# The first stage of a streaming-encoder step: shifts and scales by quarters of the channels, index keys made in it, and a gate with four weight buffers

## The chip, the cores and the metric

One core of a Trainium2 chip runs the whole step as one program. The metric is the time of one execution on the device in microseconds; 1285.39 is the median of three runs of the kernel before.

## The reference

One layer (DEPTH 1) over 1024 prompt tokens and 32 sample tokens, D = 1024 channels, everything in float32. What the change touches is the beginning and one factor at the end:

```
mod = silu(c) @ w_ada + b_ada                  # c: one row for the prompt, one for the sample
shift, scale, gate = split(mod, 3)
h = rms_norm(x, g_norm) * (1 + scale) + shift
z = h @ w_in                                   # columns: q k v gate_a iq iw ik glu gate_b merge
dots = relu(iq . ik); score = sum_heads(iw * dots); top-k keys per query; attention over them
...
x = x + gate * (mixed @ w_out); y = rms_norm(x, g_final)
```

Besides y it returns k, v, ik (the index keys) and the last rows of the convolution, for both token groups.

## The kernel before

Activations are held with channels on the partitions: xT, and h as a pair hh + hl (the rounded value and the rest), 8 blocks k of 128 channels by 1056 tokens. A product in float32 precision is three matmuls, wh by hh, wh by hl and wl by hh (mm3).

The **first stage** makes hh and hl and the first index queries. What runs in it, and in which order, stands in two lists. LOADS is the order of the loads on SP's queue: x:i is a tile of 128 tokens (x:8 the 32 sample tokens, 4 buffers), a a piece of w_ada (tiles of 1 MB, 4 buffers), q and k raw weights. ORDER is the order in which the rest is issued; PE, DVE and ACT are scheduled by hand, POOL and SP are not. Its words:
- sq:i squares x tile i with its sum (ACT, sq_x); sc:i,.. puts the small operations that turn sums into 1/rms on a list (scale_x: ACT's root between DVE's small operations, then the scaling of the tile on the engine that XENG names: tile 4 on ACT, tiles 0, 7 and 8 on POOL, the others on DVE). Two of that list are issued after each word (DRIP), all that are left before a t.
- t:i transposes tile i (8 on PE, trans_x), c:i copies the result to xT, half on DVE, half on ACT.
- m:q,i,k multiplies the 4 columns of silu(c) with block k of w_ada, for half q of the channels, i = 0 shift, 1 scale (mod); p:q,i,k,e prepares such a block as a split pair, which makes its matmuls two short ones (mod_pre); v copies a row out of PSUM, o turns it by transposes and makes AB, the scale and shift per channel (mod_row, mod_out).
- h:part,k makes hh and hl of channel block k for tokens f (0 to 255), i (256 to 767) or t (768 to 1023): h on POOL, hh on ACT, hl = h - hh on DVE (h_of); hS does it for the 32 sample tokens on DVE.
- w splits 128 columns of index-query weights (prep); q:t,c,k multiplies query tile t (two heads each) with column group c (512 or 288 columns) of block k.

Behind ORDER the two query tiles are copied out of PSUM (iq_out) and the **jobs** begin (class Jobs): one after another, a block of weight columns times all of hh and hl, 8 steps each; proj has 9 matmuls of 352 columns a step. The first job before is the index keys and head weights (72 columns), the second query tiles 2 and 3. After each step the job loop issues entries of the list side, npop of them per step (side work: transposes, the dots of the indexer, and at the end the gate). idx_done copies the index keys out, writes them twice with their split (dup), transposes them (tr) and puts the first dots on the list. The caches' keys are loaded and transposed by cache_ik ahead of the first job and by cache_kT as a side entry.

Near the end the jobs yaj multiply with w_a (8 tiles of 128 channels), with the **gate** as side work: 16 additions gate_add on DVE (each a scaled 128 x 512 block of w_ada for both token groups), then for either half a split and a row by matmuls (gate_row). The blocks are loaded by POOL's queue into 2 buffers, graw; gate_add(i) issues the load of i + 2. Its rate is 0.25 entries a step in the first of the four weight loads and 0.375 in the others. Then comes the output product y, which takes all of PSUM.

Of the kernel before, what the change touches and what calls it, by code (L numbers as in the profile page):

```python
# [107 lines left out]
def _build(tc, nc, a, o, top):  # L108
# [121 lines left out]
    def load_ada(q, i, k0, n=4):  # L230

        c = D * i + 512 * q
        src = w_ada[128 * k0:128 * k0 + 512, c:c + 512].rearrange("(k p) c -> p k c", p=128)
        t = tl(stp, [128, 4, 512], F, "ada", 4)
        for k in range(0, 4, n):
            nc.sync.dma_start(t[:, k:k + n], src[:, k:k + n])
        for k in range(4):
            ada[q, i, k0 + k] = t[:, k]
# [23 lines left out]
    nc.vector.memset(rest, 0.0)
    psS, psS_st = pool("psS", space=PSUM)
    p = tl(psS, [128, 512], F, "iq00")
    for i in range(WARM):
        nc.tensor.matmul(p, rest[:, 0:128], rest, start=True, stop=True)
    nc.vector.memset(scf, 0.0)
# [4 lines left out]
    nc.scalar.activation(sc, p.rearrange("p (s k) -> p k s", s=2), AF.Silu)  # L272
# [63 lines left out]
    pm, mrow, halves = {}, {}, {}  # L336

    def mod_pre(q, i, k, eng):
        h = tl(stp, [128, 512], FR, "ah", 2)
        l = tl(stp, [128, 512], FR, "al", 2)  # L340
        (nc.vector.tensor_copy if eng >= 2 else nc.scalar.copy)(h, ada[q, i, k])
        (nc.gpsimd if eng % 2 else nc.vector).tensor_sub(l, ada[q, i, k], f32(h))
        halves[q, i, k] = h, l

    def mod(q, i, k):

        if k == 0:
            pm[q, i] = misc([4, 512])
        out = pm[q, i]
        if (q, i, k) in halves:  # L350
            h, l = halves.pop((q, i, k))
            nc.tensor.matmul(out, sch[:, k, :], h, start=k == 0, stop=False)
            nc.tensor.matmul(out, scz[:, k, :], l, start=False, stop=k == KD - 1)
        else:
            nc.tensor.matmul(out, scf[:, k, :], ada[q, i, k], start=k == 0, stop=k == KD - 1)  # L355

    def mod_row(q, i):
        mrow[i] = tl(stp, [128, 512], F, "h", 4)[:4]
        (nc.scalar.copy, nc.vector.tensor_copy)[i](mrow[i], pm.pop((q, i)))

    def mod_out(q):
        p = misc([128, 2, 4, 4])
        for i in range(2):
            for c in range(4):
                nc.tensor.transpose(p[:, i, c, :], mrow[i][:, 128 * c:128 * c + 128], ident[:4, :4])
        j = slice(4 * q, 4 * q + 4)
        mc = tl(stp, [128, 2, 4, 2], F, "mc", 2)
        bias = bg_[:, 0:16].rearrange("p (i j) -> p i j", i=2)[:, :, j, None]
        nc.vector.tensor_add(mc, p[:, :, :, 2:4], bias.to_broadcast([128, 2, 4, 2]))
        nc.vector.tensor_add(AB[:, j, 2:4], p[:, 1, :, 0:2], mc[:, 1])  # L370
        nc.vector.tensor_mul(AB[:, j, 2:4], AB[:, j, 2:4], bg_[:, 16:24][:, j, None].to_broadcast([128, 4, 2]))
        nc.vector.tensor_add(AB[:, j, 0:2], p[:, 0, :, 0:2], mc[:, 0])

    def h_of(j, sel_):
        x, hi, lo = sel_(xT[:, j]), sel_(hh[:, j]), sel_(hl[:, j])
        h = tl(stp, [128, 512], F, "h", 4)[:, :x.shape[-1]]
        nc.gpsimd.tensor_scalar(h, x, AB[:, j, 2:3], AB[:, j, 0:1], op0=OP.mult, op1=OP.add)  # L377
# [3 lines left out]
    def h_sample():  # L381
        h = tl(stp, [128, 512], F, "h", 4)[:, :KD * TS].rearrange("p (k n) -> p k n", k=KD)
        z = slice(TP, T)
        nc.vector.tensor_mul(h, xT[:, :, z], AB[:, :, 3:4].to_broadcast([128, KD, TS]))
        nc.vector.tensor_add(h, h, AB[:, :, 1:2].to_broadcast([128, KD, TS]))
        nc.vector.tensor_copy(hh[:, :, z], h)
        nc.vector.tensor_sub(hl[:, :, z], h, f32(hh[:, :, z]))
# [3 lines left out]
    def iq_mm(t, w, ks, cs=(0, 1)):  # L391
        for k in ks:
            for c in cs:
                if k == 0 and c not in iqps[t]:
                    iqps[t][c] = tl(psS, [128, 512], F, f"iq{t}{c}")
# [3 lines left out]
                    k == 0, k == KD - 1)  # L399

    iqw = {}
    drip = []
    for op, *i in ORDER:
# [4 lines left out]
        elif op == "p":  # L408
            mod_pre(*i)
# [15 lines left out]
        elif op == "w":  # L425
            iqw[i[0]] = prep(iqraw, 128 * i[0], 128)
        elif op == "h":
            h_of(i[1], lambda x, z=part_of[i[0]]: x[:, z])
        elif op == "hS":
            h_sample()  # L430
        elif op == "q":
            iq_mm(i[0], iqw[i[0]], [i[2]], (i[1],))
        elif op == "sch":
            split(sc, sch[:, :, 0:2], sch[:, :, 2:4])
            nc.scalar.copy(scz[:, :, 0:2], sc)
# [4 lines left out]

    idv = ident.rearrange("p (a b) -> p a b", a=4)
    nc.gpsimd.tensor_add(sel[:, 0], idv[:, 0], idv[:, 1])
    nc.gpsimd.tensor_add(sel[:, 1], idv[:, 2], idv[:, 3])
    nc.gpsimd.tensor_add(sel[:, 0], sel[:, 0], sel[:, 1])
    for i in range(1, 4):
        nc.gpsimd.tensor_copy(sel[:, i], sel[:, 0])

# [80 lines left out]
    def first_w():  # L528
        h, l = [slot8(FR)[:, :KD * 72].rearrange("p (k n) -> p k n", k=KD) for i in range(2)]
        split(ikraw[:, :, :72], h, l)  # L530
        return h, l

    iq_out(0, (0,))
    first = first_w()
    iq_out(0, (1,))
    iq_out(1)
# [14 lines left out]
    class Jobs:  # L551
# [29 lines left out]
        def run(self):  # L581
# [27 lines left out]
            if evac:  # L609
# [3 lines left out]
    psS_st.close()  # L613
    psA, psA_st = pool("psA", space=PSUM)
# [748 lines left out]
    jobs = [("w", [(w_in, C_IK, 64), (w_in, C_IW, 8)], [(0, 72, idx_done)], 1, hrows),  # L1363
# [111 lines left out]
    yaj = Jobs([("w", [(a["w_a"][0], 128 * j, 256)], [(0, 128, ya_done(j)), (128, 128, ya_done(j + 1))], 0.375 if j else 0.25,  # L1475
# [95 lines left out]
    def gate_add(i):  # L1571
# [8 lines left out]
        gate_load(i + 2)  # L1580
# [149 lines left out]
```

## Time and profile before

| what | us |
|---|---|
| median of 3 runs (1285.0 to 1286.13) | 1285.39 |
| profiled execution | 1284.44 |
| its span | 1282.6 |
| TensorE busy | 1253.7 (98%) |
| DVE busy | 899.9 (70%) |
| ACT busy | 616.6 (48%) |
| POOL busy | 196.8 (15%) |

Busy shares are means over stages with different limits; TensorE's matmuls are pipelined, and their ends are modelled. The time of an instruction is its duration on its engine, x8 a run of eight put together; what ended the idle time before it stands in brackets. Groups put like instructions together.

### The profile page before, as it was taken

What the parts mean: (1) busy time and instruction counts of PE and PEld (TensorE: products, weight loads), DVE (VectorE), ACT (ScalarE), POOL (GpSimd) and SP (SyncE); (2) the same over time, 40 slices, a digit from 0 to 9 for tenths busy, and PEclk for the clock granted to TensorE, in tenths of its full rate; (3) what the DMA queues carried; (4) which work ended last, traced back from release to release, by engine and by line L of the source; (5) the groups of instructions that cost most, each with busy time, mean ns of one, the idle gap of its engine ahead of it and who ended that gap; (6) DMA issues with size and microseconds to landing.
All of it is one profiled execution on the core that took longest, in us unless ns stands there. A gap on an engine that the chain in (4) does not pass through costs nothing.

```text
span 1282.6 us, 19154 instructions
## 1 busy us (share of the span) xinstructions
PE 1253.7 (98%) x7434; PEld 1179.0 (92%) x7434; DVE 899.9 (70%) x1435; ACT 616.6 (48%) x1142; POOL 196.8 (15%) x289
## 2 busy tenths in 40 slices
PE   7899999999999999999999999999999999998997
PEld 2589999999999999999999999999998889997786
DVE  4855547878899888978875469752358888667454
ACT  5645443576676667666114243340247675115222
POOL 3730110000000000100000000000123352221222
PEclk9999999999999999999999999999999999999999
DMA  9431222131222211211222421266124326545131
GB/s 341 133 101 51 84 76 76 51 101 52 86 69 64 97 56 67 85 67 69 101 101 103 165 101 47 89 235 203 38 86 113 91 77 224 166 152 186 54 127 71
DMA packets 110395, 136.38 MB, mean 106 GB/s; under 512 B 10667, under 2 KB 87715, under 8 KB 110176
## 3 DMA queue, kind: packets, MB, share of 16 engines
q1 hardware_dynamic: 99232, 100.62, 25.0%
q10 hardware_dynamic: 5872, 19.48, 3.8%
q0 software_dynamic: 5200, 15.05, 3.6%
q8 instruction: 58, 0.95, 0.3%
q14 instruction: 33, 0.27, 0.1%
HBM read 98.60 MB, written 36.54 MB: 105 GB/s over the span
## 4 chain that ended last, share of the span: by engine, by line
PE 92%; DVE 2%; DMA 2%; POOL 2%; issue 1%; ACT 1%; ACTq 0%; SPq 0%; DVEq 0%; POOLq 0%
PE proj L545 66%; PE PT L1284 2%; PE y L130 2%; PE y L132 2%; PE y L131 2%; PE O L130 1%; PE O L132 1%; PE O L131 1%; DMA graw<-in_w_ada_dram 1%; PE misc L743 1%; PE misc L744 1%; POOL h L377 1%; PE misc L355 1%; PE misc L132 1%; PE misc L131 1%
## 5 line engine op out<-in xcount | busy, mean ns | idle before, releaser
L967 DVE SCALAR_TENSOR_TENSOR s<-u,vec,s 128x1086 f32<-128x1086 f32 x240 | 314.4, 1346 | 2.6
L545 PE MATMUL proj<-hh,wh 128*128 128x352 f32 x1440 | 312.8, 325 | 0.0
L545 PE MATMUL proj<-hh,wl 128*128 128x352 f32 x1440 | 310.3, 323 | 0.0
L545 PE MATMUL proj<-hl,wh 128*128 128x352 f32 x1440 | 309.8, 323 | 0.0
L545 PEld LDWEIGHTS proj<-hh,wh 128*128 128x128 f32 x1440 | 245.1, 189 | 1.9
L545 PEld LDWEIGHTS proj<-hh,wl 128*128 128x128 f32 x1440 | 246.8, 188 | 0.0
L545 PEld LDWEIGHTS proj<-hl,wh 128*128 128x128 f32 x1440 | 244.6, 188 | 0.0
L813 ACT ACTIVATE relu<-scores,cand 128x384 bf16<-128x384 f32 (+6 forms) x224 | 183.6, 821 | 72.1 <-DVE cand L828 69.5
L127 DVE TENSOR_TENSOR wl<-raw,wh 128x1024 fp32r<-128x1024 f32 (+1 forms) x84 | 100.7, 1202 | 79.6 <-ACT wh L126 78.4
L126 ACT CAST wh<-raw 128x1024 fp32r<-128x1024 f32 (+1 forms) x84 | 85.9, 1026 | 56.2 <-PE proj L545 44.2
L746 ACT ACTIVATE relu<-misc 128x384 f32<-128x384 f32 (+3 forms) x80 | 39.9, 523 | 63.6 <-PE misc L744 62.3
L757 DVE SCALAR_TENSOR_TENSOR scores<-relu,iws,scores 128x384 f32<-128x384 f32 (+3 forms) x70 | 43.6, 655 | 34.5 <-ACT relu L746 34.4
L126 ACT CAST u<-PT 128x512 fp32r<-128x512 f32 (+2 forms) x76 | 43.1, 571 | 45.1 <-PE PT L1284 42.9
L127 DVE TENSOR_TENSOR u<-PT,u 128x512 fp32r<-128x512 f32 (+2 forms) x76 | 50.6, 670 | 14.7 <-ACT u L126 14.3
L906 ACT ACTIVATE s<-proj 128x1056 f32<-128x1056 f32 x24 | 25.3, 1052 | 68.1 <-PE proj L545 68.1
L126 ACT CAST mh<-E 128x1056 fp32r<-128x1056 f32 x8 | 8.6, 1074 | 72.1 <-DVE E L1428 72.1
L813 ACT ACTIVATION_READ_ACCUMULATOR relu<-scores,cand 128x1 f32 x224 | 41.8, 187 | 0.0
L545 PE MATMUL proj<-oa,wh 128*128 128x352 f32 x192 | 41.7, 326 | 0.0
L1264 POOL TENSOR_SCALAR E<-E,st 128x1024 f32<-128x1024 f32 (+4 forms) x36 | 33.5, 932 | 42.0 <-DVE st L1263 22.8
L545 PE MATMUL proj<-u,wh 128*128 128x352 f32 x192 | 38.6, 322 | 0.0
L1259 ACT ACTIVATE E<-E,st 128x1024 f32<-128x1024 f32 (+4 forms) x36 | 34.7, 963 | 7.9 <-DVE st L1252 7.8
L1663 ACT ACTIVATE x<-yv 128x512 f32<-128x512 f32 (+2 forms) x19 | 11.6, 609 | 55.8 <-DVE yv L1662 55.8
(444 smaller groups left out, 2113.8 us busy)
## 6 DMA issues: line engine op xcount, KB each, us to landing
raw<-in_w_in_dram SPq DMA_DIRECT2D x24, 1024.0 KB, 5.3
raw<-in_w_in_dram SPq DMA_DIRECT2D x16, 512.0 KB, 5.2
ada<-in_w_ada_dram SPq DMA_DIRECT2D x24, 256.0 KB, 5.4
sma_d<-s ACTq DMA_DIRECT2D x8, 528.0 KB, 2.7
smb_d<-s ACTq DMA_DIRECT2D x8, 528.0 KB, 2.7
ga_d<-s ACTq DMA_DIRECT2D x8, 528.0 KB, 2.7
qh_d<-s ACTq DMA_DIRECT2D x8, 528.0 KB, 2.7
ql_d<-s SPq DMA_DIRECT2D x8, 528.0 KB, 2.8
```

The costliest lines, as they stand in the source:

```text
L126: nc.scalar.copy(hi, src)
L127: nc.vector.tensor_sub(lo, src, f32(hi))
L130: nc.tensor.matmul(out, ah, bh, start=first, stop=False)
L131: nc.tensor.matmul(out, ah, bl, start=False, stop=False)
L132: nc.tensor.matmul(out, al, bh, start=False, stop=last)
L545: nc.tensor.matmul(p[:n, c, :CH], a_[:, k, :n], b_(k, c), start=first, stop=last)
L746: nc.scalar.activation(r[:, :n], p[:, :n], AF.Relu, scale=0.125)
L757: nc.vector.scalar_tensor_tensor(acc, r[:, :n], w, acc, op0=OP.mult, op1=OP.add)
L813: nc.scalar.activation(scr[:, :s.shape[1]], s, AF.Sign, bias=f32(hold["cand"])[:, i:i + 1], accum_out=cnt[:, i:i + 1])
L967: nc.vector.scalar_tensor_tensor(d[:, :DW], u[:, k:k + DW], wj[:, k:k + 1], d[:, :DW], op0=OP.mult, op1=OP.add)
L1259: nc.scalar.activation(e, e, AF.Exp, bias=mn, scale=-1.0, accum_out=st[:, 1:2])
L1264: nc.gpsimd.tensor_scalar(e, e, st[:, 2:3], 1.0, op0=OP.mult, op1=OP.mult)
```

## The change

The shifts and scales are made by quarters of 256 channels. w_ada is loaded in tiles of 4 channel blocks by 2 x 256 columns (shift and scale side by side), 5 buffers. silu(c) is widened to 32 columns (scp, zero beyond the first two), and the four blocks of a tile are multiplied into four groups of 32 partitions of one PSUM bank, which the matmuls with sel in mod_out add while they turn the row. The split pairs (p) are gone. AB comes two channel blocks at a time, and hS as well. The index keys' product (k:, ik_mm) is in ORDER, by column groups of 352; of the index queries only tile 0 is. Tile 1 is the first job. The transposes of x use the two misc banks. idx_done is called ahead of the first job, and the caches' transposes are side entries.

```
 LOADS: x:2 a:0,0 x:3 a:0,1 x:4 x:5 q:0 a:1,0 a:1,1 x:6 x:8 x:7 k a:2,0 a:2,1 x:0 x:1 a:3,0 a:3,1 q:1
 ORDER:
+sq:2 b sc:2 t:2 c:2 m:0,0 sq:3 sc:3 t:3 c:3 m:0,1 v:0 sq:4 sc:4 o:0 t:4 c:4 w:0 sq:5 sc:5 t:5 c:5 h:i,0 h:i,1 q:0,0
+q:0,1 m:1,0 sq:6 m:1,1 v:1 sq:8 sc:6,8 o:1 t:6 t:8 c:6 c:8 h:i,2 sq:7 sc:7 h:i,3 q:0,2 t:7 c:7 h:t,0 hS:0 q:0,3
+h:t,1 hS:1 q:1,0 wk h:t,2 q:1,1 h:t,3 q:1,2 q:1,3 k:0,1,2 m:2,0 k:1,1,2 k:2,1,2 m:2,1 v:2 k:3,1,2 sq:0 o:2 sq:1
+h:i,4 sc:0,1 h:i,5 q:0,4 t:0 c:0 q:0,5 t:1 c:1 m:3,0 h:t,4 hS:2 h:t,5 q:1,4 h:f,0 q:1,5 k:4,1,2 h:f,1 k:5,1,2 h:f,2
+m:3,1 h:f,3 v:3 k:0,0 k:1,0 o:3 h:i,6,1 k:2,0 h:i,7,1 h:t,6 k:3,0 h:t,7 hS:3 h:f,4 q:0,6 h:f,5 q:0,7 q:1,6 q:1,7
+k:6,1,2 h:f,6 k:7,1,2 w:1 h:f,7 k:4,0 k:5,0 k:6,0 k:7,0
...
+    def load_ada(q, g):
+        t = ada[q, g] = tl(stp, [128, 4, 2, 256], F, "ada", 5)
+        for i in range(2):
+            c = D * i + 256 * q
+            nc.sync.dma_start(t[:, :, i], w_ada[512 * g:512 * g + 512, c:c + 256].rearrange("(k p) c -> p k c", p=128))
...
+    def mod(q, g):
+        if g == 0:
+            pm[q] = tl(psS, [128, 512], F, "acc")
+        for j in range(4):
+            nc.tensor.matmul(pm[q][32 * j:32 * j + 32], scp[:, 4 * g + j, :], ada[q, g][:, j].rearrange("p i c -> p (i c)"),
+                             start=g == 0, stop=g == 1)
...
+                nc.tensor.matmul(p[:, i, c, :], mrow[q][:, 256 * i + 128 * c:256 * i + 128 * c + 128], sel[:, 0, 0:2],
+                                 start=True, stop=True)
...
+        (nc.vector if eng else nc.gpsimd).tensor_scalar(h, x, AB[:, j, 2:3], AB[:, j, 0:1], op0=OP.mult, op1=OP.add)
...
+    def ik_mm(k, *cs):
+        wh, wl = iqw["k"]
+        for a_, b_, first, last in ((wh, hh, k == 0, False), (wh, hl, False, False), (wl, hh, False, k == KD - 1)):
+            for c in cs:
+                nc.tensor.matmul(ikp[:72, c, :CH], a_[:, k, :72], b_[:, k, CH * c:CH * c + CH], start=first, stop=last)
...
-    jobs = [("w", [(w_in, C_IK, 64), (w_in, C_IW, 8)], [(0, 72, idx_done)], 1, hrows),
+    jobs = [("w", None, [(0, 128, 1)], 1, hrows),
...
-    cache_ik()
-    side.append(cache_kT)
-    Jobs(jobs, first).run()
+    jobs = Jobs(jobs, iqw[1])
+    jobs.load(1)
+    load_caches()
+    idx_done(ikp)
+    side.extend([cache_ik, cache_kT])
...
-    yaj = Jobs([... 0.375 if j else 0.25, ...
+    yaj = Jobs([... 0.5 if j else 0.25, ...
...
-            graw[i] = tl(mx, [128, 512], F, "graw", 2)
+            graw[i] = tl(at, [128, 512], F, "gt", 2) if i & 2 else tl(mx, [128, 512], F, "graw", 2)
...
-        gate_load(i + 2)
+        if i < 2:
+            gate_load(i + 2)
+        gate_load(i + 4)
```

## Rows read from the trace of the kernel before

**Rows 1.** List of TensorE's waits: us in total, times, longest.
```profile
PE tx L327 <- DVE xt L315: 5.0, 2, 3.2
...
PE y L130 <- ACT qh L1595: 3.8, 1, 3.8
...
PE proj L545 <- ACT wh L126: 2.1, 1, 2.1
```

**Rows 2.** Chain of waits, first 160 us: start, us, what.
```profile
59.31 6.00 POOL h L377 x7
```

**Rows 3.** TensorE in order of time, first stage: start, us, instruction, idle before.
```profile
10.81 1.97 PE L327 MATMUL tx<-ident,xt 128*128 128x128 f32 x8 [3.23 <-DVE xt L315]
...
19.52 1.07 PE L327 MATMUL tx<-ident,xt 128*128 128x128 f32 x8
...
24.11 1.03 PE L327 MATMUL tx<-ident,xt 128*128 128x128 f32 x8
...
68.22 0.29 PE L132 MATMUL iq<-hh,wl 128*128 128x288 f32 x1
...
69.83 0.41 PE L646 MATMUL misc<-ident,s 128*64 128x128 f32 x2 [1.32 <-DMA s<-in_cache_idx_k_dram]
```

**Rows 4.** ACT in order of time, first stage.
```profile
19.64 1.06 ACT L293 ACTIVATE junk<-xt 128x1024 bf16<-128x1024 f32 x1 [3.66 <-DMA xt<-in_x_prompt_dram]
...
22.64 1.13 ACT L313 ACTIVATE xt<-xt,rs_r 128x1024 f32<-128x1024 f32 x1
...
45.53 0.59 ACT L333 COPY xT<-tx 128x512 f32<-128x512 f32 x1 [2.41 <-PE tx L327]
...
46.02 1.06 ACT L293 ACTIVATE junk<-xt 128x1024 bf16<-128x1024 f32 x1
```

**Rows 5.** Gate weights' tile: who stood idle before it (us, times).
```profile
  DMA graw<-in_w_ada_dram: 15.4, 4
```

**Rows 6.** TensorE in order of time, after 1138 us.
```profile
1144.56 1.08 PE L545 MATMUL proj<-oh,wh 128*128 128x352 f32 x3 [2.07 <-ACT wh L126]
```

**Rows 7.** Stretches: busy us of each engine, granted clock, DMA share, GB/s.
```profile
20.00:30.00 10.00, 10.00 (x42) 3.34 (x40) 6.25 (x18) 8.52 (x17) 5.64 (x5) 1.00 1.04 380
...
1144.00:1148.00 4.00, 3.44 (x12) 3.44 (x13) 4.00 (x6) 0.50 (x1) 2.44 (x3) 0.60 0.75 248
```

**Rows 8.** DVE in order of time, first stage.
```profile
18.62 0.75 DVE L315 TENSOR_SCALAR xt<-xt,rs_r 128x1024 f32<-128x1024 f32 x1
...
21.50 0.15 DVE L306 RECIPROCAL rs_r<-rs_s 128x1 f32<-128x1 f32 x1
...
22.26 0.16 DVE L310 TENSOR_TENSOR rs_r<-rs_r,rs_t 128x1 f32<-128x1 f32 x1
...
36.92 1.61 DVE L315 TENSOR_SCALAR xt<-xt,rs_r 128x1024 f32<-128x1024 f32 x1
```

**Rows 9.** Groups by form, first 160 us: count, busy us, mean ns, idle before.
```profile
L355 PE MATMUL misc<-ada,scf 128*4 128x512 f32 x40 | 20.1, 620 | 0.0
...
L377 POOL TENSOR_SCALAR h<-xT,AB 128x256 f32<-128x256 f32 x16 | 13.4, 850 | 5.7 <-ACT xT L333 5.7
...
L377 POOL TENSOR_SCALAR h<-xT,AB 128x512 f32<-128x512 f32 x8 | 9.4, 1172 | 2.3 <-DVE vv L303 2.0 <-DVE hl L387 0.4
...
L378 ACT ACTIVATE hh<-xT,AB 128x512 fp32r<-128x512 f32 x8 | 6.2, 802 | 0.0
...
L379 DVE TENSOR_TENSOR hl<-h,hh 128x256 fp32r<-128x256 f32 x16 | 7.7, 489 | 4.2 <-POOL h L377 4.2
...
L379 DVE TENSOR_TENSOR hl<-h,hh 128x512 fp32r<-128x512 f32 x8 | 5.8, 735 | 0.6 <-POOL h L377 0.6
```

**Rows 10.** TensorE in order of time, behind the first stage.
```profile
81.77 0.64 PE L545 MATMUL proj<-hh,s 128*72 128x352 f32 x3
...
95.52 0.39 PE L130 MATMUL proj<-hh,wh 128*128 128x512 f32 x1
...
96.61 0.39 PE L130 MATMUL proj<-hh,wh 128*128 128x512 f32 x1
```

More of the change, by code (lines that the diff above doesn't have):

```diff
@@ L228, in _build @@
     xn = {}
[L230 to L238, printed above, removed]
+    def load_ada(q, g):
[3 more added lines that the diff above has]
+            nc.sync.dma_start(t[:, :, i], w_ada[512 * g:512 * g + 512, c:c + 256].rearrange("(k p) c -> p k c", p=128))
     def load_x(i):
@@ L249, in _build @@
     nc.scalar.dma_start(brow[16:24], fold(a["g_norm"]))
-    iqraw = None
+    ikraw, iqraw = [tl(wpool, [128, KD, 256], F, "raw", 2) for i in range(2)]
     for op, *i in LOADS:
@@ L255, in _build @@
             load_ada(*i)
-        elif op == "q":
-            iqraw = load_w([(w_in, C_IQ, 256)])
-        else:
-            ikraw = load_w([(w_in, C_IK, 64), (w_in, C_IW, 8)])
+        elif op == "k":
+            for c, c0, n in ((0, C_IK, 64), (64, C_IW, 8)):
+                nc.sync.dma_start(ikraw[:, :, c:c + n], w_in[:, c0:c0 + n].rearrange("(k p) c -> p k c", p=128))
+        else:
+            c = 128 * i[0]
+            nc.sync.dma_start(iqraw[:, :, c:c + 128], w_in[:, C_IQ + c:C_IQ + c + 128].rearrange("(k p) c -> p k c", p=128))
+    idv = ident.rearrange("p (a b) -> p a b", a=4)
+    nc.gpsimd.tensor_add(sel[:, 0], idv[:, 0], idv[:, 1])
+    nc.gpsimd.tensor_add(sel[:, 1], idv[:, 2], idv[:, 3])
+    nc.gpsimd.tensor_add(sel[:, 0], sel[:, 0], sel[:, 1])
+    for i in range(1, 4):
+        nc.gpsimd.tensor_copy(sel[:, i], sel[:, 0])
     rest = tl(stp, [128, 512], BF, "junk")
@@ L263, in _build @@
     psS, psS_st = pool("psS", space=PSUM)
[L264 to L267, printed above, removed]
+    for tag in ("acc", "iq0", "iq1"):
+        tl(psS, [128, 512], F, tag)
+    ikp = tl(psS, [128, 3, 512], F, "ik")
+    scp = tl(stp, [128, KD, 32], F, "scp")
+    nc.vector.memset(scp, 0.0)
     warm = tl(stp, [128, 1], F, "warm")
@@ L334, in trans_x @@
         cops[i] = copies
[L336 to L355, printed above, removed]
@@ L357, in mod_row @@
-    def mod_row(q, i):
-        mrow[i] = tl(stp, [128, 512], F, "h", 4)[:4]
-        (nc.scalar.copy, nc.vector.tensor_copy)[i](mrow[i], pm.pop((q, i)))
+    pm, mrow = {}, {}
+    def mod(q, g):
[4 more added lines that the diff above has]
+                             start=g == 0, stop=g == 1)
+    def mod_row(q):
+        mrow[q] = tl(stp, [128, 512], F, "h", 4)
+        (nc.scalar.copy, nc.vector.tensor_copy)[q % 2](mrow[q], pm.pop(q))
@@ L361, in mod_out @@
     def mod_out(q):
-        p = misc([128, 2, 4, 4])
+        p = misc([128, 2, 2, 2])
         for i in range(2):
[L364 to L367, printed above, removed]
-        bias = bg_[:, 0:16].rearrange("p (i j) -> p i j", i=2)[:, :, j, None]
-        nc.vector.tensor_add(mc, p[:, :, :, 2:4], bias.to_broadcast([128, 2, 4, 2]))
@@ L370, in mod_out @@
[L370 to L375, printed above, removed]
+            for c in range(2):
+                nc.tensor.matmul(p[:, i, c, :], mrow[q][:, 256 * i + 128 * c:256 * i + 128 * c + 128], sel[:, 0, 0:2],
+                                 start=True, stop=True)
@@ new lines, in mod_out, with h_of @@
+        j = slice(2 * q, 2 * q + 2)
+        mc = tl(stp, [128, 2, 2, 2], F, "mc", 2)
+        bias = bg_[:, 0:16].rearrange("p (i j) -> p i j", i=2)[:, :, j, None]
+        nc.vector.tensor_add(mc, p, bias.to_broadcast([128, 2, 2, 2]))
+        nc.vector.tensor_mul(AB[:, j, 2:4], mc[:, 1], bg_[:, 16:24][:, j, None].to_broadcast([128, 2, 2]))
+        nc.vector.tensor_copy(AB[:, j, 0:2], mc[:, 0])
+    def h_of(part, j, eng=0):
+        z = part_of[part]
+        x, hi, lo = xT[:, j, z], hh[:, j, z], hl[:, j, z]
@@ L376, in h_of, with h_sample @@
         h = tl(stp, [128, 512], F, "h", 4)[:, :x.shape[-1]]
-        nc.gpsimd.tensor_scalar(h, x, AB[:, j, 2:3], AB[:, j, 0:1], op0=OP.mult, op1=OP.add)
+        (nc.vector if eng else nc.gpsimd).tensor_scalar(h, x, AB[:, j, 2:3], AB[:, j, 0:1], op0=OP.mult, op1=OP.add)
         nc.scalar.activation(hi, x, AF.Identity, bias=AB[:, j, 0:1], scale=AB[:, j, 2:3])
         nc.vector.tensor_sub(lo, h, f32(hi))
[L381 to L387, printed above, removed]
+    def h_sample(q):
+        h = tl(stp, [128, 512], F, "h", 4)[:, :2 * TS].rearrange("p (k n) -> p k n", k=2)
+        k, z = slice(2 * q, 2 * q + 2), slice(TP, T)
+        nc.vector.tensor_mul(h, xT[:, k, z], AB[:, k, 3:4].to_broadcast([128, 2, TS]))
+        nc.vector.tensor_add(h, h, AB[:, k, 1:2].to_broadcast([128, 2, TS]))
+        nc.vector.tensor_copy(hh[:, k, z], h)
+        nc.vector.tensor_sub(hl[:, k, z], h, f32(hh[:, k, z]))
@@ L426, in _build @@
             iqw[i[0]] = prep(iqraw, 128 * i[0], 128)
+        elif op == "wk":
+            iqw["k"] = prep(ikraw, 0, 72)
         elif op == "h":
-            h_of(i[1], lambda x, z=part_of[i[0]]: x[:, z])
+            h_of(*i)
         elif op == "hS":
-            h_sample()
+            h_sample(*i)
         elif op == "q":
[L432 to L435, printed above, removed]
+            iq_mm(0, iqw[0], [i[1]], (i[0],))
+        elif op == "k":
+            ik_mm(*i)
         for f in range(DRIP):
@@ L439, in _build @@
     stp_st.close()
[L441 to L446, printed above, removed]
     upool, upool_st = pool("upool")
@@ L526, in iq_out @@
         nc.gpsimd.tensor_copy(iqs[64:128, 2 * t + 1, :], f32(d[0:64, z]))
[L528 to L536, printed above, removed]
+    iq_out(0)
     def proj(w, rows, n, npop, mid):
@@ L611, in run @@
             step(0)
-    psS_st.close()
-    psA, psA_st = pool("psA", space=PSUM)
     onesr = tl(big, [128, 128], FR, "onesr")
@@ L1381, in _build @@
     jobs += yb[:3] + [("call", prelude)] + yb[3:]
-    cache_ik()
-    side.append(cache_kT)
-    Jobs(jobs, first).run()
+    jobs = Jobs(jobs, iqw[1])
[3 more added lines that the diff above has]
+    side.extend([cache_ik, cache_kT])
+    psS_st.close()
+    psA, psA_st = pool("psA", space=PSUM)
+    jobs.run()
     pop(1000)
```

41 lines of the change are left out of this document (13 added, 28 removed).

## The prediction

> **What bounds the kernel now.** I read the list of TensorE's waits first, then the chain of waits, then the order of time of each engine over the first 70 us, then the gate's rows near the end. The list [rows 1] is what matters for any change of the first stage: after that stage TensorE waits in two places only, 2.1 us for a split weight (ACT wh) and 3.8 us for a copy of the gate row (ACT qh). Between them and the first stage it is never late. A microsecond lost or won before about 80 us therefore reaches the end of the kernel whole.
>
> Inside the first stage the chain runs, at its end, along POOL's h tiles (seven of them take 6.00 us) [rows 2]. The last index-query matmul starts at 68.22; the cache keys' transposes wait until 69.83 [rows 3]; then come the 72-column index keys, whose last three matmuls start at 81.77 and take 0.48, so TensorE is free of them at 82.25 [rows 10].
>
> One more thing to see is how ACT works. At 45.53 it begins a copy for which it had stood idle 2.41 us, and only behind it, at 46.02, the square of the next x tile [rows 4]. In ORDER the square stands behind that copy, and ACT takes it there. PE, DVE and ACT run what ORDER says in that order; what stands behind a waiting entry waits too. So the new ORDER is to be followed entry by entry, and that is my working.
>
> Near the end, DVE sat idle 15.4 us in four waits for the gate's weights [rows 5]. Behind them stand the sums and splits that TensorE needs: it stops 2.07 us before 1144.56, and the next three matmuls take 1.08 where three of them took 0.64 before [rows 6, 10]; the granted clock of 1144 to 1148 is 0.60 on average, a mix of 2.4 and 1.2 GHz [rows 7]. So that stop costs 2.07 + 0.4 x 4 = 3.7 us.
>
> **Part 1, the new first stage.** What it removes on TensorE: 20 matmuls of w_ada at 1.0 us (20.1 us in 40 records) [rows 9], and 12 split pairs. What it adds: 8 groups m of four blocks. No row shows four blocks side by side. Bounds from the nearest row: one matmul's time, 1.0, if they truly overlap, 4.0 if they run one after another. I take 1.0, because the four write different partitions and each uses 32 columns; 4.0 is a rival.
>
> The Trainium skill's page "TensorE: Matmul & The Clock Gate" (Part 3, Measured speedup vs the span model) has three column blocks at 2.38 times. With the same share for four, an estimate from that page, a group would take 4.0 / 3.2 = 1.26 us, and the six groups on the chain below would add 1.6 us to the sum. No run here shows it yet.
>
> By work alone this would be a good trade. But the new ORDER says "sq:3 sc:3 t:3 c:3 ... sq:4 sc:4 ... t:4 c:4": the square of a tile stands on ACT behind the copy of the tile before, that copy waits for the transposes, and those wait for the scaling. One tile's chain is this. From the square at 19.64 [rows 4] to the end of the last small DVE operation at 22.42 is 2.78 us; the small operations among them step by 0.19 (21.50 to 22.26 in four) and take 0.92 together; the scaling is 0.75 on DVE alone and 1.61 beside POOL [rows 8], which with hand-overs makes 3.6 from square to transposes; with ACT's scaling of 1.13 it is 4.47 as measured, 19.64 to 24.11 [rows 3, 4]. The transposes take 1.05 (1.97 in the first burst) [rows 3], the copy of 512 columns 0.59 [rows 4].
>
> The chain, with the time at which each link ends (v is taken as a copy, 0.59; o as eight transposes, 1.0; the three AB operations 0.57; hS as four of 0.25, k: with two blocks 6 x 0.16 = 0.97 by [rows 10]; h, hh and hl from [rows 9]):
> - transposes of tile 2 start as before, 10.8
> - t:3: 1.97 + 0.59 + 3.6: 17.0
> - t:4: t 1.07, m 1.0, v:0 0.59 ahead of the square on ACT, 4.47: 24.1
> - t:5: 1.03, 0.59, w:0 another 1024-wide ACT pass 1.06, 3.6: 30.4
> - t:6: half of t:5 and its copy 1.1, two h on POOL 2.34, hl 0.74, q 0.47, m:1,0 and m:1,1 2.0, v:1 0.59, o:1 1.0, AB 0.57, 0.4 to the root, 0.92, scaling beside POOL 1.61, hand-overs 0.6: 42.7
> - t:7: t:6 and copy 1.64, t:8 and copy 0.5, h:i,2 0.80, sq:7 1.25, root 0.4, h:i,3 0.80, hl 0.74, 0.92, scaling on POOL as 1.61: 51.4
> - q:1,3: 1.1, h 0.85, then DVE in line: two hl, two hS, wk 0.7, two hl: 6.9 in all: 58.3
> - m:2,1: three k and two m: 63.2
> - t:0: v:2 0.59 and then both squares 2.5, two hh 1.6, root 0.2, 0.92, 1.61, hand-overs 0.5: 71.1
> - t:1 done: t, q:0,5, t: 73.9
> - m:3,1: copy 0.59, hh 0.59, hl, hS:2, hl 2.0, q 0.8, k:4 and k:5 1.94, m 1.0: 80.8
> - AB of the last quarter: v 0.59, o 1.0, 0.57, hand-overs: 83.3
> - DVE's run h, hl, h, hl, two hl, hS:3, about 4.5: 87.8
> - last matmuls q:1,6 and q:1,7 0.8, k:6 and k:7 1.94, four k of one block 1.92: 92.5
>
> Before, the same chain had other entries between its links, so that squares and scalings ran while TensorE had w_ada matmuls; here TensorE mostly stands. It will stand 3 to 5 us again and again, longer than the 2.07 behind which the granted clock was 0.60, so part of its work will run at 1.2 GHz. Some 12 us of the chain is TensorE's own before it has a long run, so between 0 and 12 is to be added; I take 5, since the k run in the middle should be at 2.4 GHz: end of the stage 97.5, bounds 92 and 105.
>
> The transfers don't bind: the stage loads some 14.1 MB, which at 380 GB/s [rows 7] is 37 us, and though x:1 and w_ada's last quarter stand in SP's queue behind t:6 (42.7), they land in the fifties, before m:3,0 asks for them after 70. Splitting w_ada's loads into 256-column rows and the index query's into 128-column rows is therefore priced at nothing; the cover is those 15 us and more. The same holds for the five-buffer ring of w_ada. POOL's operations for sel stand ahead of its first h tile, which the chain has after 30 us.
>
> **Part 2, keys in the stage, second query tile behind it.** The work is the same 8 x 6 matmuls of 1.09 us a step (95.52 to 96.61) [rows 10], now in the first job. It starts when the stage's PSUM banks are copied out: four DVE subtractions behind DVE's last hl. I take 1.5 us of wait (before: 1.32 [rows 3]; bounds 0.5 to 3). So the query tile ends at 97.5 + 1.5 + 8.7 = 107.7. Before, the same work was done at 82.25, and with it some 0.9 us of cache transposes that now come later: 81.4. Part 1 and 2 together: +26.3 us. The caches' transposes and the keys' become entries between matmuls instead of a wait; that 1.3 us is within the above.
>
> **Part 3, gate with 4 buffers, rate 0.5.** A load is now issued four additions ahead instead of two. An addition comes every 1 / 0.5 steps of 1.45 us, 2.9 us, so a load has 11.6 us instead of 2 x 3.9 = 7.7, and DVE's four waits should go. The first stop of TensorE goes with them: 3.7 us. The second, 3.77, goes because the 24 entries of the gate need 4 + 40 x 0.5 = 24, thus 40 of the 48 steps, and the last gate row is copied a whole tile before the end. Next late is then the last mixed tile (its DVE product, sum and split, some 5 us), which the first y matmuls don't need until their eighth row block: some 0.3 us remains. With the clock lost behind it, taken equal to the first, 1.6: 3.77 - 0.3 + 1.6 = 5.1. Part 3: -8.7, bounds -10 and 0. What it costs: DVE does four additions a tile instead of three, and is nearly full for three tiles; its results have a whole tile of slack.
>
> **Sum.** 26.3 - 8.7 = +17.6. The profiled execution took 1284.44 (span 1282.6 and 1.84 around it), 0.95 below the median of 1285.39. 1285.4 + 17.6 = 1303.0 us.
>
> **Rivals.**
> - Faster: the engines aren't held to the new order, or the waits overlap more than I see. Then the stage ends where its work does: TensorE's 9 x 1.05 + 8 + 4 + 8.7 + 11.5 = 42, or the last quarter of w_ada at about 41 and 12.4 us of links behind it, 54. It decides from about 72 on: 72 + 10.2 = 82.2 is 0.8 over 81.4, and the gate's gain is then nearly the whole result. At 54: 64.2 - 81.4 - 8.7 = -26, 1259 us. For it speaks that TensorE's work falls by some 13 us; against it [rows 4], and that t:4 to t:8 of the old list fall in the trace where its written order puts them. The Trainium skill's page "TensorE: Matmul & The Clock Gate" (Architectural detail) calls ACT's and DVE's queues strict FIFO, and the trace agrees with the 2.41 us. Chance 0.09.
> - The four blocks run one after another: 3.0 more for each of the six groups m on the chain: +18, 1321 us. Nothing in the trace speaks for or against. Chance 0.12.
> - The gate's stops stay, because POOL's queue holds the loads behind the copies for msl (they wait for the split): 1303 + 8.7 = 1312 us. Against it: those copies are through within 3 us of the split. Chance 0.08.
>
> **How the numbers follow.** My forecast has 0.71: 1303, of its own between 1295 and 1313 (stage end 92 to 105, gate -6 to -10). To hold 8 in 10, I go down to 1291 (a stage that ends 10 us earlier) and up to 1322, which takes in the second rival. Faster by over 0.2% (2.6 us, about what can be told from no change): 0.09; within it 0.02; slower 0.89.
>
> **What would show it.** TensorE idle ahead of t:3 to t:7 with the scaling of x as releaser, 3 us or more each; t:6 near 43 and t:0 near 71; the first query matmul of the second tile near 99 us; groups m of about 1 us (2 at 1.2 GHz), not 4; no wait of DVE for graw, and no wait before the y matmuls. If t:7 stands before 45, part 1 is wrong in its main step.

## Result and profile after

The changed kernel takes 1303.0 us (median of 4 runs, 1302.05 to 1303.24) against 1285.47 us for the kernel before, measured beside it: 1.0135 times as long, 95% interval 1.0117 to 1.0152. The prediction was 1303.0 with a range of 1291 to 1322; that the two agree to the digit is luck, as the terms below show. The profiled execution took 1303.24 with a span of 1301.3, which is 18.7 over the span before.

Where the 18.7 lie is seen by laying the same instruction of both traces side by side. In the rows PE is TensorE, DVE VectorE, ACT ScalarE and POOL GpSimd; O and PT are tiles of the attention, far behind the first stage. Before, then after:
```profile
946.14 0.39 PE L130 MATMUL O<-u,vh 128*128 128x512 f32 x1
1068.59 0.60 PE L1284 MATMUL PT<-ident,E 128*128 128x128 f32 x4
1175.07 0.50 PE L130 MATMUL y<-wh,mh 128*128 128x512 f32 x1 [3.77 <-ACT qh L1595]
```
```profile
974.90 0.39 PE L126 MATMUL O<-u,vh 128*128 128x512 f32 x1
1097.11 0.60 PE L1263 MATMUL PT<-ident,E 128*128 128x128 f32 x4
1195.80 0.39 PE L126 MATMUL y<-wh,mh 128*128 128x512 f32 x1
```
The first matmul into O stands 28.8 us later than before, the last four transposes of E into PT 28.5 later, the first y matmul 20.7 later and the end 18.7 later. So the first stage, with the second query tile behind it, lost some 28.5 us, and the gate gave 9.8 back: 7.8 ahead of the first y matmul, 2.0 behind it.

TensorE's waits, the longest groups of the list (total, times, longest); they answer to [rows 1]:
```profile
PE misc L326 <- DVE xt L314: 14.4, 4, 5.0
PE misc L326 <- POOL xt L314: 5.3, 2, 3.2
PE iq L126 <- ACT hh L368: 4.6, 4, 1.7
PE iq L126 <- DVE hh L376: 3.1, 3, 1.3
...
PE misc L326 <- ACT xt L312: 2.6, 1, 2.6
```
The two waits near the end that [rows 1] had, for wh and for the gate row, are gone. In their place the transposes of x (misc L326) wait seven times for a scaled tile (xt), 22.3 us together. TensorE's order of time shows where (start, us, instruction, idle ahead of it); it answers to [rows 3]:
```profile
15.66 1.94 PE L326 MATMUL misc<-ident,xt 128*128 128x128 f32 x8 [2.13 <-DVE xt L314]
...
23.79 1.97 PE L326 MATMUL misc<-ident,xt 128*128 128x128 f32 x8 [2.61 <-ACT xt L312]
30.79 1.94 PE L326 MATMUL misc<-ident,xt 128*128 128x128 f32 x8 [5.03 <-DVE xt L314]
...
45.63 3.25 PE L326 MATMUL misc<-ident,xt 128*128 128x128 f32 x16 [3.36 <-DVE xt L314]
55.13 1.97 PE L326 MATMUL misc<-ident,xt 128*128 128x128 f32 x8 [3.17 <-POOL xt L314]
...
65.45 1.80 PE L342 MATMUL acc<-ada,scp 128*32 128x512 f32 x8
...
69.25 1.07 PE L342 MATMUL acc<-ada,scp 128*32 128x512 f32 x8
78.28 1.97 PE L326 MATMUL misc<-ident,xt 128*128 128x128 f32 x8 [2.15 <-POOL xt L314]
...
102.92 0.47 PE L126 MATMUL proj<-hh,wh 128*128 128x512 f32 x1 [1.37 <-DVE s L507]
```
These are t:3, t:4, t:5, t:6 (with t:8), t:7, the groups m:2,0 and m:2,1, t:0, and the first query matmul of the second tile. Eight transposes take 1.07 at full clock [rows 3] and nearly twice that here. The stretches say why (busy us of PE, PEld, DVE, ACT, POOL; granted clock; DMA share; GB/s); the first answers to [rows 7]:
```profile
20.00:30.00 10.00, 2.99 (x16) 2.54 (x16) 4.08 (x18) 5.23 (x10) 0.00 (x0) 0.63 0.87 229
30.00:40.00 10.00, 7.82 (x30) 3.95 (x30) 2.72 (x4) 4.19 (x7) 1.52 (x2) 0.52 1.02 341
50.00:60.00 10.00, 5.57 (x15) 3.56 (x16) 4.51 (x15) 4.71 (x10) 2.88 (x5) 0.50 0.22 68
60.00:80.00 20.00, 15.43 (x72) 10.14 (x71) 6.40 (x22) 4.67 (x9) 5.78 (x6) 0.67 0.17 53
...
1172.00:1176.00 4.00, 4.00 (x27) 4.00 (x26) 2.82 (x4) 2.94 (x5) 1.27 (x1) 1.00 0.35 125
```
From 20 to 30 us TensorE was busy all ten before, at a clock of 1.00 [rows 7], and is busy 2.99 now. At a clock of 0.50 all of the stretch runs at 1.2 GHz. (Only for the row at 15.66 the stretches do not say it: from 10 to 20 us the trace gives 1.00, though the row is as long as those at half clock.) The last row is the place of the first stop near the end [rows 6, 7], shifted by 28: TensorE is full there now, at 2.4 GHz. At the gate's weights (tile graw), who stood idle for whom; it answers to [rows 5]:
```profile
  DVE ql L1562: 5.6, 4
```
This is POOL's queue waiting for VectorE to free a buffer. The DMA line with its 15.4 us is gone, and the two new buffers (tile gt) have none for these loads either.

### The profile page after: what moved, and what is told of

It is laid out like the page before. It is cut to its first block, busy times and chain, and to the rows that moved or that the text cites. A ratio compares the mean times of both kernels' runs of the same rounds, so it can differ in the third digit from the quotient of the medians.

```text
span 1301.3 us, 19154 instructions
## 1 busy us (share of the span) xinstructions
PE 1251.9 (96%) x7450; PEld 1184.8 (91%) x7450; DVE 894.0 (69%) x1447; ACT 615.3 (47%) x1136; POOL 180.7 (14%) x278
## 4 chain that ended last, share of the span: by engine, by line
PE 94%; DVE 2%; ACT 2%; issue 1%; POOL 0%; DMA 0%; SPq 0%; DVEq 0%; ACTq 0%; POOLq 0%
PE proj L524 68%; PE PT L1263 2%; PE y L128 2%; PE y L126 2%; PE y L127 2%; PE O L126 1%; PE O L128 1%; PE O L127 1%; PE misc L326 1%; PE misc L722 1%; PE misc L723 1%; PE misc L128 1%; PE misc L127 1%; PE misc L126 1%; PE proj L126 1%
## 5 line engine op out<-in xcount | busy, mean ns | idle before, releaser
L123 DVE TENSOR_TENSOR u<-PT,u 128x512 fp32r<-128x512 f32 (+2 forms) x76 | 50.6, 671 | 14.4 <-ACT u L122 14.1
L326 PE MATMUL misc<-ident,xt 128*128 128x128 f32 (+1 forms) x72 | 16.8, 410 | 22.4 <-DVE xt L314 14.4
L326 PEld LDWEIGHTS misc<-ident,xt 128*128 128x128 f32 (+1 forms) x72 | 13.7, 222 | 26.9 <-issue 17.2
```

Source lines behind the costliest of these rows:

```text
L123: nc.vector.tensor_sub(lo, src, f32(hi))
```

## Experiments

Each ratio is to the kernel before, measured beside it on the same chip.

**x tiles ahead.** Only ORDER differs from the changed kernel; its head:
```diff
-sq:2 b sc:2 t:2 c:2 m:0,0 sq:3 sc:3 t:3 c:3 m:0,1 v:0 sq:4 sc:4 o:0 t:4 c:4 w:0 sq:5 sc:5 t:5 c:5 h:i,0 h:i,1 q:0,0
+sq:2 b sc:2 t:2 sq:3 sc:3 c:2 m:0,0 sq:4 t:3 sc:4 c:3 m:0,1 sq:5 t:4 v:0 sc:5 c:4 o:0 w:0 sq:6 t:5 sq:8 sc:6,8 c:5
...
```


> Only the written order of the first stage differs from the changed kernel: square, scaling, transposes and copy of each x tile of the first eight stand ahead of the h, q and index-key words instead of being spread among them; the work is the same. Theory (the order makes the serial chain: a tile's square stands on ScalarE behind the copy of the tile before, its copy behind the h work of the tile before): transposes of t:6 start near 30 us instead of 45.6, those of t:0 near 47 instead of 78.3, the stage ends near 83 to 88 instead of 101.4, and the time is near 1286 (1284 to 1291). Rival, the four blocks of TensorE or the loads set the pace: the stage ends where it did, within 3 us, and the time stays at 1300 to 1303. Rival, the engines' total work is the limit: the x tiles come early but the q work piles up behind them, and the stage ends at 98 or later.

1287.17 us, ratio 1.0019 (1.001 to 1.0028). The order alone is worth some 15 us (15.8 by the medians, 14.9 by the two ratios). Two transposes and the second tile's start:
```profile
30.02 1.31 PE L326 MATMUL misc<-ident,xt 128*128 128x128 f32 x8 [2.44 <-DVE xt L314]
...
47.60 1.86 PE L326 MATMUL misc<-ident,xt 128*128 128x128 f32 x8 [2.04 <-POOL xt L314]
...
86.15 0.47 PE L126 MATMUL proj<-hh,wh 128*128 128x512 f32 x1 [1.38 <-DVE s L507]
```
t:6 at 30.0 and t:0 at 47.6 are what the theory said. Both rivals fall: neither the four blocks and the loads nor the work set the pace of the changed kernel. Now a transfer comes up as a limit for the first time; ScalarE's square of tile 6 stands behind its load:
```profile
25.20 1.06 ACT L292 ACTIVATE junk<-xt 128x1024 bf16<-128x1024 f32 x1 [4.27 <-DMA xt<-in_x_prompt_dram]
```

**The whole stage reordered.** Again ORDER alone; its head:
```diff
-sq:2 b sc:2 t:2 c:2 m:0,0 sq:3 sc:3 t:3 c:3 m:0,1 v:0 sq:4 sc:4 o:0 t:4 c:4 w:0 sq:5 sc:5 t:5 c:5 h:i,0 h:i,1 q:0,0
+sq:2 m:0,0 m:0,1 sc:2 sc:3 sq:3 t:3 sq:4 sq:5 sc:4 c:3 t:2 c:2 v:0 t:4 m:1,0 sc:5 c:4 t:5 w:0 m:1,1 c:5 v:1 sq:6 b o:0
...
```


> Only the written order of the first stage differs from the changed kernel: all words reordered, so that no engine's queue holds a word whose input is late ahead of one whose input is there (the modulation groups go as early as their transfers, the query and index-key words interleave by tile). Theory (order alone makes the stage longer than before): the stage ends near 65 to 72 us instead of 101.4, the second query tile starts there, and the time is 1264 to 1272, under both kernels. Rival, the transfers: they have 37 us of work for 14.1 MB, but land in the order in which they were issued, and a wait for the last quarter's ada holds the stage at 78 or later: 1278 or more. Rival, work: the stage ends at 85 or later whatever the order, 1285 or more.

1266.8 us (1265.44 to 1267.48), ratio 0.9856 (0.984 to 0.9873): faster than both kernels, and 36 us faster than the changed one, with the same instructions in other places. TensorE's waits, and one row of its order of time:
```profile
PE acc L342 <- DVE rs_r L305: 5.5, 1, 5.5
PE acc L342 <- DMA ada<-in_w_ada_dram: 2.6, 2, 2.4
...
PE misc L326 <- DVE xt L314: 0.7, 1, 0.7
```
```profile
66.09 0.47 PE L126 MATMUL proj<-hh,wh 128*128 128x512 f32 x1 [0.70 <-DVE s L507]
```
The 14.4 us of waits for DVE's xt have become 0.7. The second tile starts 36.8 us earlier. What bounds the stage now is told by pieces of its chain of waits (start, us, what):
```profile
3.81 8.60 DMA ada<-in_w_ada_dram
...
16.41 8.42 DMA xt<-in_x_prompt_dram
...
53.62 6.08 POOL h L367 x7
```
It is the loads in the first 25 us, a mixture of all engines up to 53, and at the end POOL's run of h tiles, as it was before the change [rows 2].

**Squares alone.** Each sq word of the changed kernel ahead of the copy or transposes of the tile before (sq:0 and sq:1 only ahead of the first k word), nothing else moved:
```diff
-sq:2 b sc:2 t:2 c:2 m:0,0 sq:3 sc:3 t:3 c:3 m:0,1 v:0 sq:4 sc:4 o:0 t:4 c:4 w:0 sq:5 sc:5 t:5 c:5 h:i,0 h:i,1 q:0,0
+sq:2 b sc:2 t:2 sq:3 c:2 m:0,0 sc:3 sq:4 t:3 c:3 m:0,1 v:0 sc:4 o:0 sq:5 t:4 c:4 w:0 sc:5 sq:6 t:5 sq:8 c:5 h:i,0
...
```


> Only the squares of the x tiles are moved in the changed kernel's written order, each ahead of the copy (or transposes) of the tile before; scaling, transposes, copies and the h, q and key words keep their order among themselves. Theory A (the square behind the copy of the tile before is the link that makes the chain, as the prediction put it first): each of seven tile links loses the 1.06 to 1.25 us of a square, the stage ends 7 to 10 us earlier, 1293 to 1296. Theory B (the scaling and the copies behind the h, q and modulation words make it; the square is a small share): t:3 and t:4 come 1 to 2 us earlier, the rest little, the stage ends 0 to 4 us earlier, 1299 to 1303.

1300.78 us, ratio 1.0123 (1.0106 to 1.014); the second tile starts at 99.14, 3.8 earlier. Theory B holds at the end of the stage, and with it a point of the prediction falls: the square, which it named first, is the link of the first steps only. Rows of ScalarE, VectorE and TensorE in this kernel:
```profile
14.11 1.06 PE L326 MATMUL misc<-ident,xt 128*128 128x128 f32 x8 [0.77 <-DVE xt L314]
...
16.82 1.05 ACT L292 ACTIVATE junk<-xt 128x1024 bf16<-128x1024 f32 x1
...
20.50 1.97 PE L326 MATMUL misc<-ident,xt 128*128 128x128 f32 x8 [2.55 <-ACT xt L312]
...
24.07 1.23 DVE L123 TENSOR_TENSOR wl<-raw,wh 128x1024 fp32r<-128x1024 f32 x1 [1.72 <-ACT wh L122]
25.21 0.15 DVE L302 TENSOR_SCALAR vv<-ss 128x1 f32<-128x1 f32 x1
...
26.60 0.75 DVE L314 TENSOR_SCALAR xt<-xt,rs_r 128x1024 f32<-128x1024 f32 x1
27.50 1.94 PE L326 MATMUL misc<-ident,xt 128*128 128x128 f32 x8 [5.03 <-DVE xt L314]
```
Nearly all of the 3.8 us is there at t:4 (20.50 instead of 23.79), more than theory B had for it; 1.55 of it came with t:3, and on the way from there to t:4 the transposes took 1.06 instead of 1.94, so that part of the gain is the clock's. Behind t:4 only 0.5 more is won. The square of tile 5 begins at 16.82. The first root operation on it (vv) is taken up at 25.21, over seven us after the square's end, because on VectorE it stands behind the copy c:4 and behind the split wl, which itself waits 1.72 for ScalarE. From t:4 to t:5 it is 7.0 us here (20.50 to 27.50) as in the changed kernel (23.79 to 30.79). There the square of tile 5 ends at 28.4 and the split at 28.6: two links that end almost together, so taking one away shows the other. The Trainium skill's page "TensorE: Matmul & The Clock Gate" (Part 1, Architectural detail) says that ScalarE's and VectorE's queues are strictly first in, first out; these rows agree, with work of 0.15 us held back by seven.

**Blocks in turn.** The four blocks of a group into the same 32 rows, one after another (the copy and the turn of the row then take these 32 rows alone):
```diff
-nc.tensor.matmul(pm[q][32 * j:32 * j + 32], scp[:, 4 * g + j, :], ...
-                 start=g == 0, stop=g == 1)
+nc.tensor.matmul(pm[q][0:32], scp[:, 4 * g + j, :], ...
+                 start=g == 0 and j == 0, stop=g == 1 and j == 3)
```


> The four blocks of a modulation group go into the same 32 rows of PSUM and are summed there, one matmul after the other, instead of into four row groups side by side; everything else, the number of matmuls too, is as in the changed kernel. Theory (side by side they take the time of one): a group takes 3 to 4 us at full clock instead of 1.07, 8 groups 18 to 24 us more of TensorE; of this what stands on the chain of the stage is seen, 4 to 15 us, so 1307 to 1318. Rival, the groups lie in TensorE's waits for the x tiles: below 3 us, under 1306. Rival, a busier TensorE has its full clock sooner and this pays for it: 1303 or less.

1318.39 us, ratio 1.0262 (1.0246 to 1.0277): 15.4 us over the changed kernel (1303.0). A group at full clock, and the start of the second tile, 15.0 later than in the changed kernel:
```profile
18.23 3.62 PE L342 MATMUL acc<-ada,scp 128*32 128x512 f32 x8
...
117.90 0.47 PE L126 MATMUL proj<-hh,wh 128*128 128x512 f32 x1 [1.36 <-DVE s L507]
```
3.62 in turn against 1.07 side by side, 3.4 times: the four do run together.

**Fillers.** 134 bf16 matmuls of 384 columns (a tile for 512 columns doesn't fit into SBUF beside the stage's), read by nobody, in TensorE's waits; the first form, and the form without its side effect:
```diff
+        elif op == "f":
+            fill(*i)      # n matmuls of 384 columns into a bank not yet in use
+            continue      # second form only
...
-sq:2 b sc:2 t:2 c:2 m:0,0 sq:3 sc:3 t:3 ...
+sq:2 b sc:2 t:2 c:2 m:0,0 sq:3 sc:3 f:11 t:3 ...
```


> The changed kernel with 134 bf16 matmuls of 384 columns whose result nobody reads, put ahead of eleven entries at which TensorE waited (t:3 to t:7, t:0, and five q entries), so many that they fill about the wait; the written order of the real work is the same. Theory (the waits drop the granted clock to half and this adds some 5 us to the stage): TensorE's transposes and modulation groups between 20 and 90 us take their full-clock times (1.07 instead of 1.94), the stage ends 3 to 9 us earlier, 1294 to 1300. Rival (the clock costs nothing on the chain, since the chain is ScalarE, VectorE and GpSimd): within 2 us of 1303, or later by what fillers overrun their waits.

> The filler kernel again, with one side effect taken out: VectorE's small root operations of the next x tile are issued two after each entry of the written order, and the filler entries counted as such, so these operations came up to one entry earlier; here they come where the changed kernel has them. Theory (the granted clock alone gave the gain): 1291 to 1295, as with the filler before. Rival (the earlier root operations gave part of it): 1296 or more.

1292.91 us, ratio 1.0062 (1.0047 to 1.0077), and 1293.5 us, ratio 1.0068 (1.0053 to 1.0083). The side effect had no part that can be told from the spread. In the second form nothing of the real work is earlier in any queue, and yet 9.5 us are gone by the medians (8.6 by the two ratios). In the second form, t:4, t:5, the second tile's start, and a stretch:
```profile
22.97 1.09 PE L326 MATMUL misc<-ident,xt 128*128 128x128 f32 x8 [0.48 <-ACT xt L312]
29.09 1.06 PE L326 MATMUL misc<-ident,xt 128*128 128x128 f32 x8 [0.64 <-DVE xt L314]
...
92.15 0.47 PE L126 MATMUL proj<-hh,wh 128*128 128x512 f32 x1 [1.37 <-DVE s L517]
```
```profile
20.00:40.00 20.00, 17.19 (x112) 10.16 (x112) 9.63 (x32) 8.81 (x17) 3.02 (x4) 1.00 1.04 317
```
The clock is 1.00 and transposes take 1.06 to 1.09; the stage ends 10.8 us earlier (102.92 to 92.15). This is the price of 1.2 GHz on the chain: the waits are still there, filled with work that nobody needs, and only the rows behind them are shorter.

**Keys last.** All k words to the end of ORDER (edit: those words, in their order, cut and put at the end).


> All 16 index-key words of the changed kernel's first stage moved to its end, in the same order among themselves; nothing else is moved. Theory (the stage's chain is made by the x tiles, and the keys lie partly on it, partly in its waits): m:2,1 comes 3 to 5 us earlier, t:0 near 74 instead of 78, and 20 us of keys follow behind the last query word at 2.4 GHz, of which more was hidden before than is now saved: the stage ends 0 to 5 us later, 1303 to 1308. Rival (the keys made in the stage are what lengthens it): their 20.3 us stand whole on the chain anyway, and moving them changes nothing: 1301 to 1304 with t:0 where it was, or earlier by 5 or more if the clock gains from the unbroken run.

1307.17 us, ratio 1.0176 (1.0155 to 1.0198); t:0 and the second tile's start:
```profile
73.46 1.97 PE L326 MATMUL misc<-ident,xt 128*128 128x128 f32 x8 [2.14 <-POOL xt L314]
...
103.78 0.40 PE L126 MATMUL proj<-hh,wh 128*128 128x512 f32 x1
```
The first theory's numbers came: t:0 at 73.46 instead of 78.28, and 4 us more at the end by the medians. The profiled execution, with 1304.40 the shortest of the four, has only 0.9 of them at the second tile's start and 1.2 at its end; where the others lose the rest, no trace shows. So the keys are not what lengthens the stage; in it they take little more or less than behind it.

**The gate alone, and its two edits apart**, on the kernel before:
```diff
-    yaj = Jobs([... 0.375 if j else 0.25,
+    yaj = Jobs([... 0.5 if j else 0.25,          # rate
...
-            graw[i] = tl(mx, [128, 512], F, "graw", 2)
+            graw[i] = tl(at, [128, 512], F, "gt", 2) if i & 2 else tl(mx, [128, 512], F, "graw", 2)   # buffers
...
-        gate_load(i + 2)
+        if i < 2:
+            gate_load(i + 2)
+        gate_load(i + 4)
```


> The kernel before with the gate's edits alone: four buffers for the gate's raw tiles and the rate of the loads at 0.5; the first stage is that of before. Theory (the two parts add up): the stretch from the first y matmul's wait to the end is 9 to 10 us shorter, as in the changed kernel against the kernel before (28.5 later at the end of PT, 18.7 later at the end), 1275 to 1277. Rival, the gate gains only because the changed first stage moves its loads: 1282 to 1286.

> The kernel before with the gate's rate alone raised from 0.375 to 0.5; two buffers as before. Theory (a load has 7.7 us from two additions ahead, and needs more; a faster rate asks for it after 5.8 us): VectorE still waits for the raw gate tiles, longer per wait (4 to 6 us instead of 3.9), TensorE's first stop stays or grows, the second (3.8 us before y) goes because the gate starts its additions earlier: 1279 to 1285. Rival (the rate is what gains, as the gate's last row is early): 1275 to 1277 as both edits together.

> The kernel before with the gate's four buffers alone; the rate stays at 0.375. Theory (the waits for loads delay the additions, and through them both of TensorE's stops): VectorE's 15 us of waits for the raw tiles go, the first stop goes (3.7 us), the second shrinks from 3.8 to 1 to 3 us because the additions no longer slip but still end in the last quarter of the projection: 1278 to 1282. Rival (buffers are the whole gain): 1275 to 1277. Rival (the rate alone counts): 1284 to 1286.

Both: 1275.45, ratio 0.993 (0.9915 to 0.9945). Rate alone: 1280.59, 0.9964 (0.9951 to 0.9977). Buffers alone: 1281.05, 0.9971 (0.9958 to 0.9983). TensorE's waits near the end: with the buffers alone, from its order of time, and with the rate alone, two of the three rows that its list of waits has there, and who stood idle ahead of the gate's tiles:
```profile
1171.82 0.50 PE L130 MATMUL y<-wh,mh 128*128 128x512 f32 x1 [3.77 <-ACT qh L1597]
```
```profile
PE proj L545 <- DVE wl L127: 0.9, 1, 0.9
PE misc L1593 <- DVE graw L127: 0.9, 1, 0.9
```
```profile
  DMA graw<-in_w_ada_dram: 9.6, 6
```
The buffers take the first stop away and leave the second to the hundredth at 3.77; the rate takes the second away, and in place of the first leaves a wait of 0.9 for a split weight and two of 0.8 and 0.9 for the split of the gate row. I had expected two things that didn't come: that the second stop would shrink with the buffers, and that with the rate alone VectorE would wait longer for the tiles (4 to 6 us each) and the first stop would stay or grow. VectorE waits 9.6 us in six, 1.6 each, instead of 15.4 in four, and behind waits of 0.9 the clock stays at 1.00; why the waits are shorter was not tested. Each edit removes a stop of its own, and the gains add within their intervals (3.7 and 4.1 alone, 9.4 together; the small waits are gone with both).

**Reordered stage with fillers**, 32 of them ahead of m:0,0, m:0,1 and q:0,0.


> The fully reordered first stage, with 32 bf16 matmuls of 384 columns whose result nobody reads ahead of its three longest waits (13 ahead of m:0,0, 5 ahead of m:0,1, 14 ahead of q:0,0). Theory (the half clock still costs the reordered stage what its doubled rows show: 3.87, 1.94, 1.94, 3.04 and 1.93 us between 14 and 39 us, half of it 6.4): 3 to 6 us under the reordered kernel, 1261 to 1264, the second query tile at 60 to 63 us. Rival (the reordered stage waits for its transfers and for the other engines there): within 2 us of 1267.

1265.17 us, ratio 0.9855 (0.9838 to 0.9871), not to be told from 0.9856: the theory missed and the rival holds. The rows have full-clock times and the second tile starts 1.7 earlier, but the chain is made of loads:
```profile
15.62 8.94 DMA xt<-in_x_prompt_dram
...
34.10 9.70 DMA ada<-in_w_ada_dram
```
Where TensorE is not on the chain, its clock costs little: here at most the 1.7.

## Why the prediction was right, and where only its sum was

**The chain of the first stage: right in its links.** At full clock it was put at 92.5. The filler kernel shows the stage at full clock, and its second tile waits 1.37 before 92.15, which gives 90.8. Link by link (filler kernel; predicted start or end): t:4 22.97 (24.1), t:5 29.09 (30.4), t:6 41.16 (42.7), t:7 49.58 (51.4), m:2,1 done 61.9 (63.2), t:0 69.85 (71.1), m:3,1 done 79.1 (80.8). All of these come 1.1 to 1.8 earlier than predicted, and 0.8 of that is there at the start, at the transposes of tile 2 (10.03; 10.8 "as before"); no link by itself is off by more than 0.7. What was wrong is the reason given first, the square behind the copy: moving all the squares gave 2.2 us (3.7 between the profiled spans), moving the scalings, transposes and copies with them some 15. From t:4 to t:5 the rows show what stands in the square's place, the root operations behind the copy and the split on VectorE; how much of the 15 is theirs, and how much the transposes' and copies', no run separates. Of the signs that the prediction named, the waits ahead of t:3 and t:4 were shorter than its 3 us (2.13 and 2.61), and t:6, t:0 and the second tile came 3 to 7 us later than its 43, 71 and 99.

**The clock: mis-sized.** The term was 5 with bounds of 0 and 12; it measured 10.8. Up to t:7 the loss against the filler kernel is 5.5 (55.13 against 49.58), about the 5 that were taken. The step "the k run in the middle should be at 2.4 GHz" failed: 2.9 more are lost up to the end of m:2,1, where m:2,0 still took 1.80 and the granted clock was 0.67 from 60 to 80, and 2.3 more behind t:0. Together with the links 1.7 too long this puts the second tile at 102.92 where 99.0 was expected.

**Part 2: the wait was 1.37 (1.5 taken).** At the later anchors the kernel is 28.5 to 28.8 behind, where +26.3 was predicted. By the tile's start alone it would be 102.92 + 8.7 - 81.4 = +30.2. The remaining 1.5 is won behind that start: from 82.25 before and 102.92 now to the first matmul into O, TensorE waits no more than 0.6 in either kernel, and this takes 863.9 and 872.0, so 8.1 more, where the prediction had 8.7 for the tile and 0.9 for the later transposes. The difference is the same in every trace (863.9 with the old first stage, 871.9 to 872.2 with the new one in any order). It isn't the 1.32 wait for the caches [rows 3], which lies ahead of 82.25 and so within the 81.4; its cause stays open.

**Part 3: -8.7 predicted, -9.8 in the trace, -9.4 alone.** The stops were right in kind and in what removes each: 3.7 for the first (buffers: 3.7), 5.1 for the second (rate: 4.1 with the small waits it leaves, 5.7 on top of the buffers). The rival in which the stops stay, because POOL's queue holds the loads, did not come.

So the sum of +17.6 fits (18.7 between the profiled spans, 17.5 between the medians) because errors cancel: the clock was 5.8 too low, the links 1.7 and the work behind the stage 1.5 too high, which leaves the stage some 2.3 too low, and the gate's gain was 1.1 too low. The fit is better than its terms.

**Groups m: 1.0 taken, 1.07 measured at full clock**, in two of the eight; the others took 1.5 to 1.9. Four blocks gain 3.62 / 1.07 = 3.4 times. The rival of blocks in turn had +18; the kernel that does so is +15.4. The estimate from the Trainium skill's page "TensorE: Matmul & The Clock Gate" (Part 3, Measured speedup vs the span model) was 3.2 times, 1.26 for a group; the rows come out a little better.

**The rival on the other side** needed engines that aren't held to the order; the stage would end where its work does, at 54. They are held to it: it took a new order to bring the second tile to 66.1, and the time to 1266.8.

**Transfers at nothing: right for this order.** They appear as the limit only when the order is mended.

## What to carry to other kernels

When the order of work is written out by hand, follow each engine's queue word by word: less work on every engine can still take longer (VectorE is busy 894.0 us instead of 899.9, GpSimd 180.7 instead of 196.8, TensorE and ScalarE a little less too), and here the same instructions spanned 102.9 or 66.1 us by their order alone. Give short operations that release other engines (a root on 128 numbers, a scaling) a place ahead of long ones that are themselves late. Waits of 2 to 5 us on TensorE were paid twice where TensorE is on the chain, once as the wait and once in the rows behind it at 1.2 GHz (10.8 us in this stage); in the reordered stage, where loads are the chain, the second payment could not be measured in the medians.

## What the runs showed that was not expected

Matmuls that nobody reads, put into TensorE's waits, made the changed kernel 9 to 10 us faster, as they kept the granted clock at 1.00 from 20 us on; in the reordered stage the same trick gave nothing that can be measured. And the two gate edits turned out nearly independent: the buffers took the first of two stops 30 us apart and left the second at 3.77 to the hundredth, and the rate took the second and left three waits of 0.8 to 0.9 in place of the first.
